# A hybrid decoder trunk on one core: the bias table's DMA in eight pieces, VectorE one tile behind ScalarE at the borders, the norms' sums later

## The chip, the core and the metric
The kernel runs on one core of one Trainium2 chip. The metric is the device time of one execution in microseconds (us). A trace of one execution on the chip is read below; its times count from the span's start.

## The reference
The input is x of 512 tokens by 1024 features in float32. Two layers run, each a half-weighted SwiGLU, a mixer, and another half-weighted SwiGLU, each behind an RMSNorm; the second layer's mixer is B. A final RMSNorm ends it.

```python
def rmsnorm(x, g):
    y = xf * lax.rsqrt(jnp.mean(xf * xf, axis=-1, keepdims=True) + EPS)
    return (y * g).astype(x.dtype)

def swiglu(x, w_in, w_out):                       # D = 1024, D_FF = 2816
    gate, up = jnp.split(x @ w_in, 2, axis=-1)
    return (jax.nn.silu(gate) * up) @ w_out

h = x
for i in range(2):
    h = h + 0.5 * swiglu(rmsnorm(h, norm_g[i, 0]), ffn_w_in[i, 0], ffn_w_out[i, 0])
    hn = rmsnorm(h, norm_g[i, 1])
    y = mixer_a(hn, ..., rel_table) if i == 0 else mixer_b(hn, ...)
    h = h + y
    h = h + 0.5 * swiglu(rmsnorm(h, norm_g[i, 2]), ffn_w_in[i, 1], ffn_w_out[i, 1])
return rmsnorm(h, final_g)
```

Mixer A projects to queries, keys and values of 8 heads and to an index score, keeps the top 128 keys of each query, adds a bias `rel_table[bucket(distance)]` of each head to the logits, and applies softmax and an output projection. Mixer B is a gated MLP with a layer norm and a 128 x 128 spatial product.

## The kernel before
Activations lie transposed: `H[j]`, j = 0 to 7, holds features 128j to 128j+127 on the partitions and the 512 tokens along the row. A matrix product in float32 is made of three products of rounded parts (`mul3`): weights `whi`, `wlo` and activations `xh`, `xl` (or `yh`, `yl`). ScalarE makes a high part, VectorE the low part as value minus high part (lines 173 and 176 for weights, 295 and 296 for activations).

**Weights.** All weights lie in DRAM as one stream of loads of 512 KB (128 rows of 4 KB). SyncE's queue fetches them in order into four buffers `raw` and two `r22`; `_convert_to` makes their parts about two units ahead. Eight tiles of 128 x 128 are one unit. In each FFN the first products are plain; the others are nine blocks of two column pairs by a seven-product scheme, whose four loads are first added and subtracted by VectorE (line 152 adds two of them into `wsum`). [...]

**The start.** During the first FFN's plain products `bias_rows` makes the bias row of each head (`rows`, 8 partitions of 640 floats); line 641 lets GpSimd's DMA queue copy each row 128 times into the DRAM tensor `dist` (8 x 128 x 640 floats). Mixer A reads slanted windows of it some 480 us later (line 818). After the plain products of the first FFN, `scale` and `spread` make the norm's token scale: TensorE sums squares (line 366), VectorE runs twelve small operations of a reciprocal square root (`rsqrt`, lines 282 to 287), TensorE spreads the result over the partitions (line 374), ScalarE reads it (377, 378).

**Borders between stages.** At an FFN's end each output tile j is added to `H[j]` by VectorE (`add`, lines 608 and 609: line 608 reads, and so frees, the PSUM bank), then `finish` calls `prepare(j)` for the next stage: ScalarE makes `xh` and the square, VectorE makes `xl` (296) and adds the square to `sqacc` (307). PSUM banks come in two groups of four, `acc` and `aux`. The next stage's first group again takes four banks of the group that tiles 4 to 7 have just used. In mixers A and B the norm's sum and its reciprocal square root are taken in the wide form (`token_scale`, lines 317 to 324), after step k = 1 of the first group (`hooks={1: scale}`); in the later FFNs `scale` comes after step 3 and `spread` after step 5 of the first group's eight.

**The end.** The last FFN's output product runs in two halves of 256 tokens. Tiles 0 to 3 of a half come from one group in four `aux` banks, tiles 4 to 7 one by one in `acc` banks. `norm_scale` and `norm_rest` of the first half were called from `finish` after tiles 4 and 5 of the second half; `norm_rest` multiplies on GpSimd (line 1104) and writes the output.

Of the kernel before, what the change touches and what calls it, by code (L numbers as in the profile page):

```python
# [19 lines left out]
P = 128  # L20
# [210 lines left out]
def tile_trunk(ctx: ExitStack, tc, specs_out, xT, wst, gT, rel, onehot, bu, bv, lng, lnb, wspT, bsp, out):  # L231
# [21 lines left out]
    def bank(tag="acc"):  # L253
        return psum.tile([P, 512], F32, tag=tag, bufs=4, name=uname(tag))
# [43 lines left out]
    def square(j, s=slice(0, S), adder=nc.vector):  # L298
# [5 lines left out]
        else:  # L304
            sq = small.tile([P, S], F32, tag="s0_512", bufs=1, name=uname("sq"))
            nc.scalar.activation(sq[:, s], H[j][:, s], AF.Square)
            adder.tensor_tensor(acc[0][:, s], acc[0][:, s], sq[:, s], op=ALU.add)

    def prepare(j, norm):
        weigh(j, norm)  # L310
        square(j)

    def token_scale(tag="aux"):

# [63 lines left out]
        nc.scalar.activation(rh, ps, AF.Copy, scale=0.5)  # L378
        return rb, rh

    def ffn(layer, which, norm, finish, begin=None, hooks=None, parts=1):

# [6 lines left out]
        with tc.tile_pool(name=uname("ffn"), bufs=1) as fp:  # L391
# [144 lines left out]
            def hook(k):  # L536
                if hooks:
                    hooks[k]()
                elif k in (3, 5):
                    (scale if k == 3 else spread)()  # L540
                if k > 4 and not hooks:
                    sums(k - 5)

# [30 lines left out]
            for ci, dps in enumerate(CHUNKS):  # L574
                p0 = done
                if ci:
                    Y.clear()
                done += 2 * dps
                if ci == 0:
                    done += PLAIN  # L580
                for i in range(dps):
                    pair = PLAIN + 2 * n_dp
                    between = ()
                    if n_dp == 0:
                        between = [lambda: plain_pairs(rest, g[1], 1 if hooks else 0)]
                    two_pairs(pair, "aux" if n_dp % 2 else "acc", between)
                    n_dp += 1
                flush()
                n_k = done - p0
                tag0 = "aux" if n_dp % 2 else "acc"  # L590
                tag1 = "acc" if n_dp % 2 else "aux"

                def spec_out(k, c, p0=p0):
                    return ("ffn_w_out", (layer, which), (p0 + k) * P, [(0, c * P, P)])

                end = ci == len(CHUNKS) - 1
                if end:
                    W.spool = None
                n = S // (parts if end else 1)
                for at in range(0, S, n):  # L600
                    s = slice(at, at + n)

                    def y_parts(k):
                        return Y[k // 2][0][:, k % 2, s], Y[k // 2][1][:, k % 2, s]

                    def add(j, ps):
                        t = gate_tile()[:, 0]
                        nc.vector.tensor_tensor(t[:, s], ps[:, s], R["h"][:, s], op=ALU.mult)  # L608
                        nc.vector.tensor_tensor(H[j][:, s], H[j][:, s], t[:, s], op=ALU.add)
                        if end:  # L610
                            finish(j, s)

                    first = [bank(tag0) for _ in range(4)]
                    group([ps[:, s] for ps in first], range(4), n_k, spec_out, y_parts)
                    for j in range(4):
                        add(j, first[j])
                    for j in range(4, KD):
                        ps = bank(tag1)
                        single(ps[:, s], j, n_k, spec_out, y_parts)
                        add(j, ps)  # L620
# [7 lines left out]
    def bias_rows(rel_sb, oh_sb, oh):  # L628

        rows = bp.tile([HEADS, TBW], F32, name="rows")  # L630
        rh = bp.tile([BUCKETS, HEADS], F32R, name="rh")
        rl = bp.tile([BUCKETS, HEADS], F32R, name="rl")
        nc.scalar.activation(oh, oh_sb, AF.Copy)
        split(rel_sb, rh, rl)
        for s in (slice(0, TBW // 2), slice(TBW // 2, TBW)):
            ps = bank("aux")
            mm(ps[:HEADS, :TBW // 2], rh, oh[:, s], start=True, stop=False)
            mm(ps[:HEADS, :TBW // 2], rl, oh[:, s], start=False, stop=True)
            nc.vector.tensor_copy(rows[:, s], ps[:HEADS, :TBW // 2])
        d = dram.tile([HEADS, P, TBW], F32, name="dist")  # L640
        nc.gpsimd.dma_start(d, rows.unsqueeze(1).broadcast_to([HEADS, P, TBW]))
        return d

    def mixer_a(dist, next_norm):
        QI0 = 3 * D
# [8 lines left out]
        with ExitStack() as stack:  # L654
# [14 lines left out]

            kw = bank()  # L670
            pq = [bank("aux") for _ in range(4)]
            group([kw] + pq, ["kw"] + [QI0 + P * i for i in range(4)], KD, spec_a, hooks={1: scale})
            rb = R["b"]

            QK = {}
# [234 lines left out]
    def mixer_b(next_norm):  # L910
        with tc.tile_pool(name="mixb", bufs=1) as bp:
# [12 lines left out]
            with tc.tile_pool(name="mixbv", bufs=1) as vp:  # L924
# [10 lines left out]
                for c in range(6):  # L935
                    tag = "aux" if c % 2 else "acc"
                    banks = [bank(tag) for _ in range(NT)]
                    for k in range(KD):
                        wh, wl = W.take(*[("b_w_in", (0,), k * P, [(0, BH + c * 512 + i * P, P)]) for i in range(4)])
                        for t in range(NT):  # L940
                            xh, xl = XH[k][:, t * P:(t + 1) * P], XL[k][:, t * P:(t + 1) * P]
                            mm(banks[t], xh, wh, start=k == 0, stop=False)  # L942
                            mm(banks[t], xl, wh, start=False, stop=False)  # L943
                            mm(banks[t], xh, wl, start=False, stop=k == KD - 1)  # L944
                        if c == 0 and k == 1:
                            R["b"] = token_scale()
                        if c == 0 and k == KD - 1:
                            R["c"] = as_columns(R["b"])
                        if c == 1 and k == 3:
                            for g2 in range(2):  # L950
                                ps = bank("acc")
                                mm(ps, ones, wT.rearrange("p g t -> p (g t)")[:, g2 * 512:(g2 + 1) * 512],
                                   start=True, stop=True)
                                nc.scalar.activation(wsum.rearrange("p g t -> p (g t)")[:, g2 * 512:(g2 + 1) * 512],
                                                     ps, AF.Copy)
# [81 lines left out]
    def into(norm):  # L1037
        return lambda j, s: prepare(j, norm)

    def behind(k):  # L1040
        if k + 1 < KD:
            weigh(k + 1, 0)
        square(k)
        if k == 3:
            dist.append(bias_rows(*table))

    W.first_half()
    weigh(0, 0)
    with tc.tile_pool(name="bias", bufs=1) as bp:
# [4 lines left out]
            table.extend(load_table(oh_sb.bitcast(F32)))  # L1054
            table.append(oh)

        ffn(0, 0, 0, into(1), begin, {k: lambda k=k: behind(k) for k in range(KD)})
    mixer_a(dist[0], 2)
    ffn(0, 1, 2, into(3))
    ffn(1, 0, 3, into(4))  # L1060
    mixer_b(5)
# [5 lines left out]
    def finish(j, s):  # L1067
# [4 lines left out]
                sq.append(small.tile([P, S], F32, tag="s1_512", bufs=1, name="last_sq"))  # L1072
            nc.scalar.activation(sq[0][:, s], H[j][:, s], AF.Square)
        nc.scalar.activation(H[j][:, s], H[j][:, s], AF.Copy, scale=g_sb[:, 6, j:j + 1])
        if s.start and j in (4, 5):
            (norm_scale if j == 4 else norm_rest)(slice(0, s.start), False)

    R = {}

    def norm_scale(s, end):  # L1080
        sums = [bank("aux") for _ in range(nt)]
        for part in (acc[0], sq[0]):
            for t in range(nt):
                at = s.start + t * P
# [5 lines left out]

    def norm_rest(s, end):
        rc = R["c"]
        ps = bank("aux")
        for t in range(nt):
            at = s.start + t * P
            mm(ps[:, at:at + P], rc[:, t:t + 1].broadcast_to([P, P]), ident, start=True, stop=True)
# [8 lines left out]
            queue = nc.gpsimd if not end else nc.sync if j % 2 else nc.scalar  # L1105
            queue.dma_start(out[j, :, s], o)

    ffn(1, 1, 5, finish, parts=parts)
    tail = slice(S - S // parts, S)
    norm_scale(tail, True)  # L1110
    norm_rest(tail, True)
# [51 lines left out]
```

## Time and profile before

| what | value |
|---|---|
| time, median of 3 runs (lowest to highest) | 2173.39 us (2172.07 to 2173.98) |
| time of the profiled execution | 2170.78 us |
| its span, first to last instruction | 2169.0 us |
| mean granted TensorE clock | 0.985 |
| TensorE busy | 2091.4 us, 96% |
| VectorE busy | 1504.3 us, 69% |
| ScalarE busy | 899.8 us, 41% |

The span is what the trace covers; the time of the profiled execution is 1.8 us longer and lies 2.6 us under the median of the three runs. Busy shares are means over stages, so what a stage waits for has to be read in that stage.

### The profile page before, as it was taken

How to read it: one execution, taken by the hardware profiler on the slowest of the kernel's cores; microseconds unless marked ns; L12 is line 12 of the kernel's file. 1: busy time of each engine (PE TensorE's matmuls, PEld its weight loads, DVE VectorE, ACT ScalarE, POOL GpSimd, SP SyncE). 2: the span in 40 equal slices, each digit the busy share in tenths (PEclk: the TensorE clock that was granted, in tenths of full speed). 3: DMA queues.
4: the chain of work that ended last, by engine and by line, in shares of the span. 5: the costliest groups of instructions: out<-in, count | busy, mean ns of one | idle time of the engine just before them, and what ended most of it. 6: DMA issues, size and time to landing. Idle time of an engine off the chain costs nothing.

```text
span 2169.0 us, 29975 instructions
## 1 busy us (share of the span) xinstructions
PE 2091.4 (96%) x12344; PEld 1855.5 (86%) x12344; DVE 1504.3 (69%) x2052; ACT 899.8 (41%) x1163; POOL 91.7 (4%) x76
## 2 busy tenths in 40 slices
PE   7799999899999999998999999999999999999995
PEld 6689998788888999897889998788888888999894
DVE  4868686678667678675968686645846467687675
ACT  4535344343445445353635344322323245344353
POOL 0000000044210000000000000000000000000002
PEclk9799999999999999999999999999999999999998
DMA  6323222232112232222233222422222223222231
GB/s 184 88 99 117 98 98 78 78 110 95 69 68 99 98 117 90 105 98 78 90 105 117 98 98 78 147 88 90 87 104 89 88 88 107 98 98 103 93 117 68
DMA packets 59848, 212.32 MB, mean 98 GB/s; under 512 B 7280, under 2 KB 8368, under 8 KB 59584
## 3 DMA queue, kind: packets, MB, share of 16 engines
q1 hardware_dynamic: 56448, 201.35, 26.6%
q0 software_dynamic: 2688, 8.54, 1.9%
q8 instruction: 96, 1.57, 0.3%
q10 hardware_dynamic: 576, 0.52, 0.1%
q14 instruction: 40, 0.33, 0.0%
HBM read 205.67 MB, written 4.72 MB: 97 GB/s over the span
## 4 chain that ended last, share of the span: by engine, by line
PE 84%; DVE 8%; ACT 4%; issue 2%; DMA 2%; POOL 0%; SPq 0%; POOLq 0%; ACTq 0%; DVEq 0%
PE acc L338 14%; PE acc L339 14%; PE acc L340 14%; PE aux L340 10%; PE aux L338 10%; PE aux L339 10%; DVE wlo L176 2%; DMA raw<-in_wst 2%; ACT whi L173 2%; PE acc L942 1%; PE aux L942 1%; PE aux L943 1%; PE aux L944 1%; PE acc L943 1%; PE acc L944 1%
## 5 line engine op out<-in xcount | busy, mean ns | idle before, releaser
L176 DVE TENSOR_TENSOR wlo<-raw,whi 128x1024 fp32r<-128x1024 f32 (+1 forms) x389 | 471.9, 1218 | 286.6 <-ACT whi L173 282.1
L173 ACT ACTIVATE whi<-raw 128x1024 fp32r<-128x1024 f32 (+1 forms) x416 | 433.5, 1050 | 485.4 <-PE acc L339 216.3
L338 PE MATMUL acc<-xh,whi 128*128 128x256 f32 (+1 forms) x888 | 307.2, 346 | 11.7 <-ACT xh L295 6.3
L339 PE MATMUL acc<-xl,whi 128*128 128x256 f32 (+1 forms) x888 | 297.2, 335 | 0.3 <-DVE xl L296 0.3
L340 PE MATMUL acc<-xh,wlo 128*128 128x256 f32 (+1 forms) x888 | 297.0, 334 | 0.0
L338 PEld LDWEIGHTS acc<-xh,whi 128*128 128x128 f32 x888 | 170.1, 192 | 30.3 <-DVE gate L608 6.5
L338 PE MATMUL aux<-xh,whi 128*128 128x256 f32 (+1 forms) x592 | 191.7, 324 | 1.9 <-ACT rh L378 1.9
L340 PE MATMUL aux<-xh,wlo 128*128 128x256 f32 (+1 forms) x592 | 191.5, 324 | 0.7 <-DVE wlo L176 0.7
L339 PE MATMUL aux<-xl,whi 128*128 128x256 f32 (+1 forms) x592 | 191.3, 323 | 0.0
L338 PE MATMUL acc<-th,whi 128*128 128x256 f32 x640 | 182.5, 285 | 5.9 <-ACT u L490 5.9
L339 PEld LDWEIGHTS acc<-xl,whi 128*128 128x128 f32 x888 | 170.2, 192 | 18.3 <-DVE xl L296 1.5
L340 PEld LDWEIGHTS acc<-xh,wlo 128*128 128x128 f32 x888 | 169.9, 191 | 16.8
L339 PE MATMUL acc<-tl,whi 128*128 128x256 f32 x640 | 182.3, 285 | 0.0
L340 PE MATMUL acc<-th,wlo 128*128 128x256 f32 x640 | 182.1, 285 | 0.0
L338 PE MATMUL acc<-yh,whi 128*128 128x512 f32 (+1 forms) x376 | 143.0, 380 | 2.4 <-ACT whi L173 2.4
L339 PE MATMUL aux<-tl,whi 128*128 128x256 f32 x512 | 145.1, 283 | 0.0
L340 PE MATMUL aux<-th,wlo 128*128 128x256 f32 x512 | 145.1, 283 | 0.0
L338 PE MATMUL aux<-th,whi 128*128 128x256 f32 x512 | 145.1, 283 | 0.0
L340 PE MATMUL acc<-yh,wlo 128*128 128x512 f32 (+1 forms) x376 | 142.5, 379 | 2.3 <-DVE wlo L176 2.3
L340 PE MATMUL aux<-yh,wlo 128*128 128x512 f32 (+1 forms) x376 | 141.7, 377 | 2.3 <-DVE wlo L176 2.3
L338 PE MATMUL aux<-yh,whi 128*128 128x512 f32 (+1 forms) x376 | 141.7, 377 | 1.5 <-ACT whi L173 1.5
L339 PE MATMUL acc<-yl,whi 128*128 128x512 f32 (+1 forms) x376 | 142.2, 378 | 0.0
(261 smaller groups left out, 4396.4 us busy)
## 6 DMA issues: line engine op xcount, KB each, us to landing
raw<-in_wst SPq DMA_DIRECT2D x378, 512.0 KB, 3.2
dist<-rows POOLq DMA_DIRECT2D x1, 2560.0 KB, 55.6
h<-in_xT SPq DMA_DIRECT2D x8, 256.0 KB, 6.6
tb<-dist POOLq DMA_DIRECT2D x8, 256.0 KB, 3.9
bias<-in_bv POOLq DMA_DIRECT2D x1, 1536.0 KB, 7.5
out<-h POOLq DMA_DIRECT2D x8, 128.0 KB, 2.0
raw<-in_wst SPq DMA_DIRECT2D x2, 256.0 KB, 3.5
wT<-in_wspT POOLq DMA_DIRECT2D x1, 512.0 KB, 9.3
```

The costliest lines, as they stand in the source:

```text
L173: self.nc.scalar.activation(hi[:, s], src[:, s], AF.Copy)
L176: self.lo_engine.tensor_tensor(lo[:, s], src[:, s], hi[:, s].bitcast(F32), op=ALU.subtract)
L338: mm(ps, wh, xh, start=first, stop=False, **kw)
L339: mm(ps, wh, xl, start=False, stop=False, **kw)
L340: mm(ps, wl, xh, start=False, stop=last, **kw)
L942: mm(banks[t], xh, wh, start=k == 0, stop=False)
L943: mm(banks[t], xl, wh, start=False, stop=False)
L944: mm(banks[t], xh, wl, start=False, stop=k == KD - 1)
```

## The change
Three things change. The copy of the bias rows to DRAM is cut into eight DMAs, one for each head, which stand in the program ahead of the first FFN's blocks 1 to 8. In `prepare`, ScalarE's two operations of tile j are followed by VectorE's two operations of tile j-1, and the two squares alternate between two buffers. The norms are asked for later: after step 4 instead of 1 in the mixers, after 5 and 7 instead of 3 and 5 in the later FFNs, and in the last FFN the first half's norm moves from tiles 4 and 5 of the second half to steps 2 and 5 of that half's first group, with its banks in `acc`.

```diff
+    behind_it = []
     def prepare(j, norm):
-        weigh(j, norm)
-        square(j)
+        g = g_sb[:, norm, j:j + 1]
+        nc.scalar.activation(XH[j], H[j], AF.Copy, scale=g)
+        if j == 0:
+            acc[0] = small.tile([P, S], F32, tag="acc", bufs=1, name=uname("sqacc"))
+            nc.scalar.activation(acc[0], H[j], AF.Square)
+        else:
+            sq = small.tile([P, S], F32, tag=f"s{j % 2}_512", bufs=1, name=uname("sq"))
+            nc.scalar.activation(sq, H[j], AF.Square)
+        def rest():
+            nc.vector.scalar_tensor_tensor(XL[j], H[j], g, XH[j].bitcast(F32), op0=ALU.mult, op1=ALU.subtract)
+            if j:
+                nc.vector.tensor_tensor(acc[0], acc[0], sq, op=ALU.add)
+        behind_it.append(rest)
+        while len(behind_it) > (j < KD - 1):
+            behind_it.pop(0)()
...
-                elif k in (3, 5):
-                    (scale if k == 3 else spread)()
+                elif k in (5, 7):
+                    (scale if k == 5 else spread)()
...
+                    if aside:
+                        aside(n_dp)
                     two_pairs(pair, "aux" if n_dp % 2 else "acc", between)
...
-                    group([ps[:, s] for ps in first], range(4), n_k, spec_out, y_parts)
+                    group([ps[:, s] for ps in first], range(4), n_k, spec_out, y_parts,
+                          hooks=mids if at else {})
...
-        d = dram.tile([HEADS, P, TBW], F32, name="dist")
-        nc.gpsimd.dma_start(d, rows.unsqueeze(1).broadcast_to([HEADS, P, TBW]))
-        return d
+        return rows, dram.tile([HEADS, P, TBW], F32, name="dist")
+    def spread_bias(rows, d, h):
+        nc.gpsimd.dma_start(d[h:h + 1], rows[h:h + 1].unsqueeze(1).broadcast_to([1, P, TBW]))
...
-            group([kw] + pq, ["kw"] + [QI0 + P * i for i in range(4)], KD, spec_a, hooks={1: scale})
+            group([kw] + pq, ["kw"] + [QI0 + P * i for i in range(4)], KD, spec_a, hooks={4: scale})
...
-                        if c == 0 and k == 1:
+                        if c == 0 and k == 4:
                             R["b"] = token_scale()
...
-        ffn(0, 0, 0, into(1), begin, {k: lambda k=k: behind(k) for k in range(KD)})
+        ffn(0, 0, 0, into(1), begin, {k: lambda k=k: behind(k) for k in range(KD)},
+            aside=lambda i: 0 < i <= HEADS and spread_bias(*dist, i - 1))
...
-        if s.start and j in (4, 5):
-            (norm_scale if j == 4 else norm_rest)(slice(0, s.start), False)
...
-        sums = [bank("aux") for _ in range(nt)]
+        sums = [bank("aux" if end else "acc") for _ in range(nt)]
...
-    ffn(1, 1, 5, finish, parts=parts)
+    head = slice(0, S // parts)
+    ffn(1, 1, 5, finish, parts=parts, mids={2: lambda: norm_scale(head, False), 5: lambda: norm_rest(head, False)})
```

How the program's order moves, at three places. First GpSimd's queue around the copy of the bias rows; `yl` is the buffer that holds the one-hot table, and in brackets stands what semaphore a row waits for (`DMASW0` to `DMASW2` are those of GpSimd's first three DMAs, whose second and third are the first two rows here). Before, and after:

```order
L624 DMA rel_sb<-in_rel 32x8
L625 DMA yl_148<-in_onehot 32x640
L641 DMA dist<-rows 1024x1x640 [waits DVE_49]
L661 MEMSET caus 128x128 [waits DMASW2_49,DMASW3_49,DMASW1_49,DMAHW3_49,DVE_49,DMAHW7_49,PE_49,Activation_49]
L662 AFFINE_SELECT caus<-caus 128x128 [waits Pool_49]
```

```order
L646 DMA rel_sb_150<-in_rel 32x8
L647 DMA yl_15_148<-in_onehot 32x640
L665 DMA dist_264<-rows_250 128x1x640 [waits DVE_49]
L665 DMA dist_264<-rows_250 128x1x640 x4
L665 DMA dist_264<-rows_250 128x1x640 [waits DMASW0_49]
L665 DMA dist_264<-rows_250 128x1x640 [waits DMASW1_49]
L665 DMA dist_264<-rows_250 128x1x640 [waits DMASW2_49]
```

One DMA of 1024 copies has become eight of 128 copies each; only the first still waits for VectorE's copy into `rows`, four wait for nothing, and the last three wait for the ends of the queue's first three loads.

Next VectorE at the border between the second and the third FFN, around tiles 5 and 6 (`h_76`, `h_77`). Before, and after:

```order
L176 TENSOR_TENSOR wlo_8942<-raw_8747,whi_8941 128x1024
L608 TENSOR_TENSOR gate_8959<-acc_8934,rh_5902 128x512
L609 TENSOR_TENSOR h_76<-h_76,gate_8959 128x512
L296 SCALAR_TENSOR_TENSOR xl_93<-h_76,g_sb,xh_85 128x512
L307 TENSOR_TENSOR sqacc_8875<-sqacc_8875,sq_8964 128x512
L176 TENSOR_TENSOR wlo_8981<-raw_8814,whi_8980 128x1024
L608 TENSOR_TENSOR gate_8992<-acc_8967,rh_5902 128x512
L609 TENSOR_TENSOR h_77<-h_77,gate_8992 128x512
L296 SCALAR_TENSOR_TENSOR xl_94<-h_77,g_sb,xh_86 128x512
L307 TENSOR_TENSOR sqacc_8875<-sqacc_8875,sq_8997 128x512
L608 TENSOR_TENSOR gate_9019<-acc_9000,rh_5902 128x512
```

```order
L176 TENSOR_TENSOR wlo_8947<-raw_8754,whi_8946 128x1024
L629 TENSOR_TENSOR gate_8964<-acc_8939,rh_5969 128x512
L630 TENSOR_TENSOR h_76<-h_76,gate_8964 128x512
L323 SCALAR_TENSOR_TENSOR xl_92<-h_75,g_sb,xh_84 128x512
L325 TENSOR_TENSOR sqacc_8881<-sqacc_8881,sq_8935 128x512
L176 TENSOR_TENSOR wlo_8986<-raw_8821,whi_8985 128x1024
L629 TENSOR_TENSOR gate_8997<-acc_8972,rh_5969 128x512
L630 TENSOR_TENSOR h_77<-h_77,gate_8997 128x512
L323 SCALAR_TENSOR_TENSOR xl_93<-h_76,g_sb,xh_85 128x512
L325 TENSOR_TENSOR sqacc_8881<-sqacc_8881,sq_8968 128x512
L629 TENSOR_TENSOR gate_9024<-acc_9005,rh_5969 128x512
L630 TENSOR_TENSOR h_78<-h_78,gate_9024 128x512
```

Behind the addition to `h_76` stood `xl_93` and the square of the same tile; now those of the tile before it (`xl_92`) stand there.

Last VectorE in the last FFN. Before, between tiles 4 and 5 of the second half:

```order
L608 TENSOR_TENSOR gate_18589<-acc_18566,rh_15336 128x256
L609 TENSOR_TENSOR h_75<-h_75,gate_18589 128x256
L307 TENSOR_TENSOR sqacc_18307<-sqacc_18307,sq_18592 128x256
L1088 TENSOR_SCALAR v_18602<-aux_18596 128x1
L1088 TENSOR_SCALAR v_18602<-aux_18597 128x1
L282 TENSOR_SCALAR nwi_18605<-v_18602 128x2
L283 TENSOR_SCALAR nwy_18607<-nwi_18605 128x2
```

And after, between tile 7 of the first half (`h_78`) and the second half:

```order
L629 TENSOR_TENSOR gate_18453<-acc_18434,rh_15403 128x256
L630 TENSOR_TENSOR h_78<-h_78,gate_18453 128x256
L176 TENSOR_TENSOR wlo_18464<-raw_18285,whi_18463 128x1024
L176 TENSOR_TENSOR wlo_18492<-raw_18343,whi_18491 128x1024
L1110 TENSOR_SCALAR v_18513<-acc_18507 128x1
L1110 TENSOR_SCALAR v_18513<-acc_18508 128x1
L282 TENSOR_SCALAR nwi_18516<-v_18513 128x2
L283 TENSOR_SCALAR nwy_18518<-nwi_18516 128x2
```

The first half's reciprocal square root moved from behind the second half's tile 4 to ahead of the second half's tiles, behind two conversions of weights.

## Rows read from the trace of the kernel before

**Rows 1.** the page's head and its first two sections: the span, each engine's busy time (share of the span) and instructions, and the TensorE clock granted in 40 equal slices of the span, in tenths of full speed.
```profile
span 2169.0 us, 29975 instructions
...
PE 2091.4 (96%) x12344; PEld 1855.5 (86%) x12344; DVE 1504.3 (69%) x2052; ACT 899.8 (41%) x1163; POOL 91.7 (4%) x76
...
PEclk9799999999999999999999999999999999999998
```

**Rows 2.** for whom TensorE waited, over the whole span: us in total, times, longest us.
```profile
PE aux L374 <- DVE nwy L287: 15.5, 1, 15.5
PE aux L1096 <- DVE nwy L287: 11.0, 2, 6.4
...
PE acc L320 <- ACT ah L317: 6.0, 1, 6.0
...
PE acc L942 <- DVE gate L608: 5.4, 2, 3.5
```

**Rows 3.** stretches of the span: us, busy us of each engine (x instructions), then the granted TensorE clock (1.00 is 2.4 GHz, 0.50 is 1.2 GHz), the mean busy share of the 16 DMA engines and GB/s.
```profile
10.00:20.00 10.00, 9.71 (x42) 7.43 (x42) 7.30 (x12) 6.60 (x12) 0.00 (x0) 1.00 0.98 379
...
50.00:60.00 10.00, 0.00 (x0) 0.00 (x0) 2.27 (x2) 1.01 (x2) 0.00 (x0) 0.72 0.50 83
60.00:70.00 10.00, 3.33 (x11) 2.88 (x12) 9.24 (x24) 5.73 (x9) 0.00 (x0) 0.50 0.50 85
...
397.00:402.00 5.00, 3.58 (x8) 2.50 (x9) 4.01 (x7) 0.64 (x2) 0.00 (x0) 0.50 0.59 202
1007.00:1013.00 6.00, 4.04 (x9) 2.74 (x10) 4.35 (x8) 2.93 (x5) 0.00 (x0) 0.50 0.26 87
```

**Rows 4.** timeline of TensorE, at the places where it waited (the row at 1390.59 waited for nothing): start us, us, engine, line, operation, tiles [idle before <- who ended it].
```profile
64.76 2.05 PE L374 MATMUL aux<-ident,nwy 128*128 128x128 f32 x8 [15.53 <-DVE nwy L287]
68.72 0.80 PE L338 MATMUL aux<-xh,whi 128*128 128x512 f32 x1 [1.90 <-ACT rh L378]
...
397.69 0.80 PE L320 MATMUL acc<-ah,ones_r 128*128 128x512 f32 x1 [6.03 <-ACT ah L317]
399.22 0.80 PE L321 MATMUL acc<-al,ones_r 128*128 128x512 f32 x1 [0.74 <-DVE al L318]
...
995.65 0.50 PE L338 MATMUL acc<-yh,whi 128*128 128x512 f32 x1 [0.63 <-ACT whi L173]
...
996.91 0.50 PE L340 MATMUL acc<-yh,wlo 128*128 128x512 f32 x1 [0.52 <-DVE wlo L176]
...
1007.14 0.79 PE L338 MATMUL acc<-xh,whi 128*128 128x512 f32 x1 [3.58 <-DVE gate L608]
...
1010.61 0.80 PE L338 MATMUL acc<-xh,whi 128*128 128x512 f32 x1 [1.82 <-DVE gate L608]
...
1390.59 0.60 PE L330 MATMUL aux<-ident,nwy 128*128 128x128 f32 x4
...
2129.88 0.39 PE L338 MATMUL aux<-yh,whi 128*128 128x256 f32 x1 [1.54 <-ACT whi L173]
...
2161.00 1.22 PE L1096 MATMUL aux<-ident,nwy 128*128 128x128 f32 x4 [4.56 <-DVE nwy L287]
```

**Rows 5.** timeline of VectorE, same columns: its wait at the start, the first and the last of the twelve operations of the wide norm in mixer A, one tile's operations at the border at 1003 us, and one operation of the last norm.
```profile
57.73 1.23 DVE L152 TENSOR_TENSOR wsum<-raw,raw 128x1024 f32<-128x1024 f32 x1 [18.17 <-DMA raw<-in_wst]
...
62.28 0.15 DVE L368 TENSOR_SCALAR vcol<-aux 128x4 f32<-128x4 f32 x1
...
400.05 0.69 DVE L323 TENSOR_SCALAR ms<-acc 128x512 f32<-128x512 f32 x1 [0.89 <-PE acc L321]
...
407.52 0.69 DVE L287 SCALAR_TENSOR_TENSOR nwy<-nwt,nwy 128x512 f32<-128x512 f32 x1
...
1003.79 0.75 DVE L296 SCALAR_TENSOR_TENSOR xl<-h,g_sb,xh 128x512 fp32r<-128x512 f32 x1 [0.79 <-ACT xh L295]
...
1005.26 1.22 DVE L176 TENSOR_TENSOR wlo<-raw,whi 128x1024 fp32r<-128x1024 f32 x1
1006.40 0.68 DVE L608 TENSOR_TENSOR gate<-acc,rh 128x512 f32<-128x512 f32 x1
...
1008.60 0.75 DVE L296 SCALAR_TENSOR_TENSOR xl<-h,g_sb,xh 128x512 fp32r<-128x512 f32 x1 [0.79 <-ACT xh L295]
...
2157.08 1.25 DVE L285 TENSOR_TENSOR nwt<-nwy 128x2 f32<-128x2 f32 x1
```

**Rows 6.** DMA queues of the stretch 50:60: packets, MB, share of the time of all 16 engines (q0 is GpSimd's queue, q1 SyncE's).
```profile
q0 software_dynamic: 94, 0.48, 41.7%
q1 hardware_dynamic: 94, 0.35, 8.6%
```

**Rows 7.** DMA issues of the whole span: tiles, queue, operation, times, KB each, median us from issue to landing.
```profile
raw<-in_wst SPq DMA_DIRECT2D x378, 512.0 KB, 3.2
dist<-rows POOLq DMA_DIRECT2D x1, 2560.0 KB, 55.6
```

**Rows 8.** the chain of waits in the stretch 40:110, one piece of it: start us, us, what.
```profile
28.89 28.75 DMA raw<-in_wst
```

**Rows 9.** the DMA issue that writes the tensor dist: line, engine, operation, times, duration ns min/median/max, first and last start us.
```profile
L641 POOL DMA_DIRECT2D dist<-rows x1: 1079/1079/1079, 21.6 to 21.6; - x1
```

**Rows 10.** timeline of SyncE's queue: the two issues of weight loads ahead of the one at 28.89; start us, us, queue, line, operation, tiles.
```profile
22.44 0.33 SPq L105 DMA_DIRECT2D raw<-in_wst  x1
...
28.51 0.33 SPq L105 DMA_DIRECT2D raw<-in_wst  x1
```

More of the change, by code (lines that the diff above doesn't have):

```diff
@@ L379, in scale_rows, with ffn @@
         return rb, rh
-    def ffn(layer, which, norm, finish, begin=None, hooks=None, parts=1):
+    def ffn(layer, which, norm, finish, begin=None, hooks=None, parts=1, aside=None, mids={}):
         NJ = DFF // P
@@ L1044, in behind @@
         if k == 3:
-            dist.append(bias_rows(*table))
+            dist.extend(bias_rows(*table))
     W.first_half()
@@ L1055, in begin @@
             table.append(oh)
-        ffn(0, 0, 0, into(1), begin, {k: lambda k=k: behind(k) for k in range(KD)})
-    mixer_a(dist[0], 2)
+        ffn(0, 0, 0, into(1), begin, {k: lambda k=k: behind(k) for k in range(KD)},
+            aside=lambda i: 0 < i <= HEADS and spread_bias(*dist, i - 1))
+    mixer_a(dist[1], 2)
     ffn(0, 1, 2, into(3))
@@ L1092, in norm_rest @@
         rc = R["c"]
-        ps = bank("aux")
+        ps = bank("aux" if end else "acc")
         for t in range(nt):
```

## The prediction
> **What bounds the kernel now.** The page's head comes first: TensorE is busy 2091.4 of 2169.0 us, and its clock is near full nearly throughout [rows 1]. So VectorE's or ScalarE's time matters only where TensorE waits for it, and the next view is for whom TensorE waits [rows 2]. Four of its entries touch this change: 15.5 us for the norm's scale in the first FFN, 11.0 us in two pieces for the last norms, 6.0 us at mixer A's entry, 5.4 us at mixer B's. Third, the table of stretches: after three of these waits TensorE runs at 0.50 of its clock [rows 3]. A full stream of plain products takes 9.71 us / 42 = 0.231 us each; at 397 us one takes 3.58 / 8 = 0.448, at 1007 us 4.04 / 9 = 0.449. So a stall costs itself and then about 0.22 us for each of the next eight or nine products. The timeline gives each wait its place [rows 4].
>
> The first wait is not made by VectorE's arithmetic. VectorE stands 18.17 us at line 152 for a weight load, and the norm's twelve small operations stand behind that addition in its queue; the first of them starts at 62.28, and TensorE goes on at 64.76 [rows 4, 5]. The load was issued at 28.89 and needed 28.75 us [rows 8], against a median of 3.2 for all 378 loads; the copy of the bias table is in the queues in the meantime, 2560 KB in 55.6 us [rows 7]. From 50 to 60 us both queues moved 94 packets each, strictly by turns; the mean share of the 16 engines was 0.50 [rows 3, 6]. That is eight engines, all busy: 160 us x 0.417 / 94 = 0.71 us for a table packet of 5.1 KB, 160 x 0.086 / 94 = 0.15 us for a weight packet of 4 KB. The table goes at 0.48 MB / 10 us = 48 GB/s.
>
> **The change part by part: the table.** The words say "by heads during the blocks", and this decides the sum. The order of GpSimd's queue shows that nothing holds the pieces until the blocks: the first waits for VectorE's copy as before, four for nothing, three for loads at the queue's start. No piece uses anything a block makes. At about 1.08 us per issue, all eight stand in the queue by about 30 us, the first at 21.6 as now [rows 9]. What does change is their shape. Before, the slowest dimension had 8 entries (one source row each) and eight engines were at work. A piece has 128 copies of one row, as many as the 128 rows of a weight load, and such loads fill all 16 engines (share 0.98 at 379 GB/s) [rows 3]. So I expect the pieces on all 16 engines, one source row at a time, and every packet of a weight load then alternates with a table packet, where before half the engines were free.
>
> [...]
>
> The unknown is how fast one row of SBUF can be read. No row shows it; the bounds are 48 GB/s, if all eight rows shared one ceiling that one row can use alone, and 48 / 8 = 6 GB/s, if each row had its own. I take 24, between them: it is what one engine moves in a full stream (379 / (16 x 0.98) = 24.2) [rows 3], and what a group of four rows got of the 48. Then the table takes 2.62 MB / 24 = 109 us, from about 23.3 to 132 us, and a packet on each of 16 engines 5.12 KB x 16 / 24 = 3.41 us. A weight load is 128 packets, eight on an engine: 8 x (3.41 + 0.15) = 28.5 us each while the table runs. The load that VectorE waits for is third in the queue, behind those issued at 22.44 and 28.51 [rows 10]: 23.3 + 3 x 28.5 = 109 us if the turns are strict, and 132 at the latest, when the table ends. I take 120 instead of 28.89 + 28.75 = 57.6: **+62 us** (51 to 74). Everything behind it (7 us of VectorE up to 64.76, then the half clock) follows as now, and the loads after it come at their own 3.2 us once the table is through.
>
> [...]
>
> **The borders.** At the border into the third FFN VectorE idles 0.79 us in every tile, because line 296 wants a high part that ScalarE has only begun [rows 5]. One tile behind, that operand is ready: 8 x 0.79 = 6.3 us of VectorE's queue go, and line 608, which frees the banks, comes earlier by them. The waits to go are 3.58 + 1.82 for banks and 0.63 + 0.52 for weights' parts queued behind the same idling [rows 4], and the half clock, 9 x 0.218 = 2.0: together 8.5. The 6.3 us of VectorE cover the longest single wait with room. Mixer B's entry shows the same two waits (5.4, longest 3.5) [rows 2]; taken alike, 8.5. Mixer A's entry has 6.03 + 0.74 for the wide norm's input [rows 4], 8 x 0.217 = 1.7 of clock, and I take the same 1.15 for weights: 9.6. Asking for the sum after step 4 instead of 1 is what removes the 6.03. What is late next is the end of that chain: twelve wide operations, from 400.05 to 408.21, 8.2 us [rows 5], must fit in the three steps that remain. In mixer A a step is 15 products, three are 45 x 0.231 = 10.4 us: fits. In mixer B a step is 12 products, three are 8.3 us for 8.2 of chain and some more ahead of it, where before nothing waited (1390.59) [rows 4]: I charge 0.4. In the later FFNs, the small norm two steps later lies under the products of the first group: 0, plus or minus 1. Sum of the borders: 9.6 + 8.5 + 8.1 = **26** (20 to 29).
>
> **The end.** Of the 11.0 us at line 1096 the 6.4 is the first half's norm, asked for between two tiles [rows 2]; at step 5 of a group it has products around it. The 4.56 at 2161 stays [rows 4], but GpSimd's multiplications of the first half end some 11 us earlier, and with them what stretches the last norm's small operations (1.25 us for 128 x 2 at 2157.08, where 128 x 4 took 0.15 at 62.28) [rows 5], two of them on the path: 2 more. Against that, step 2 of the second half must wait for the last square of the first, near the wait of 1.54 for weights at 2129.88 [rows 4], and first-half norm operations now stand ahead of those conversions: 2 to 3 lost. Sum: **5** (2 to 8).
>
> Sum against the profiled execution, span 2169.0 and 1.8 around it: 2170.8 + 62 - 26 - 5 = 2202. It lies 2.6 under the median, so I write 2203.
>
> **Rivals.** *B, the start stays as it is*, the pieces being handled on eight engines at the old rate: nothing in the queue's order speaks against that, the slowest dimension does. 2171 - 31 = 2140. *C, the 48 GB/s can be had from one row:* a packet takes 5.12 x 16 / 48 = 1.71 us, a load 8 x 1.86 = 14.9, the third lands between 23.3 + 44.6 = 68 and 78, the table's end: +15, so 2155. *D, the start's wait vanishes:* a piece on one engine leaves 15 to the weights, or the pieces are held back after all until the blocks have room. Then 15.53 + 1.90 and some 3 of half clock go too [rows 4]: 2171 - 31 - 20 = 2120. *E, one row gives 6 GB/s:* the table lasts 437 us, and each load 8 x 13.8 = 110; far over 2400. The side changes where the third load lands 31 us later, at 89: three loads in 66 us is 2.74 us a pair of packets, 2.6 for the table's, which one row at 82 / 2.6 = 32 GB/s would give. Above that the change is faster, below it slower.
>
> **How the numbers follow.** My forecast has 0.58: the packets by turns are measured, 16 engines are what shape and rows say, but the row's rate is chosen. B 0.13, C 0.12, D 0.13, E 0.04. A measurement of this kernel tells 0.2%, 4 us, from no change. Faster: B, D and nearly all of C, 0.36; same 0.02, the long end of C; slower 0.62. The range leaves out D and E: 2136, B with borders 4 better, to 2235, a row's rate of about 20 (table end at 154, load near 140, +82 less 25 and a few). My forecast's own range is 2185 to 2220.
>
> **What would show it.** In the queues of 50 to 60 us: DMA share near 1.00 instead of 0.50, table packets on GpSimd's queue at about 3.4 us, 24 GB/s. VectorE's wait at line 152 of about 80 us instead of 18.17, TensorE's at line 374 (now 392) of about 77. Table pieces issued within 10 us of 21.6. At the borders no wait of TensorE for line 608's successor, 629, and its clock full. Wrong if the pieces' issue times lie at the blocks, if the share stays at 0.50 with 48 GB/s, or if one row gives over 32 GB/s.

## The result: 2200.3 us, slower by 1.3%

The changed kernel takes 2200.29 us (median of 4 runs, 2199.63 to 2205.22) against 2173.68 before (median of 4, 2172.07 to 2174.23): 26.6 us more. The ratio over all runs is 1.0129, 95% interval 1.0111 to 1.0146. The forecast was 2203.

The profiled execution, below, took 2205.2 us, the longest of the four and 4.9 over their median; that of before lies 2.9 under its median of four. So the two traces differ by 34.5 us where the medians differ by 26.6. The head of its page, as in [rows 1]:

```profile
span 2203.5 us, 29993 instructions
...
PE 2092.6 (95%) x12344; PEld 1856.9 (84%) x12344; DVE 1500.8 (68%) x2052; ACT 899.4 (41%) x1163; POOL 94.8 (4%) x83
```

The work is the same; TensorE is busy 2092.6 us as before. The span has grown by 34.5 us, nearly all of it waiting. For whom TensorE waited (us in total, times, longest), as in [rows 2]; line 392 was 374, 356 was 338, 629 was 608, 965 was 942, 1118 was 1096, and 338 and 339 were 320 and 321:

```profile
PE aux L392 <- DVE nwy L287: 65.7, 1, 65.7
...
PE acc L356 <- ACT whi L173: 5.1, 2, 4.6
PE acc L356 <- DVE gate L629: 3.0, 2, 1.6
PE acc L965 <- DVE gate L629: 3.0, 2, 1.6
...
PE aux L1118 <- DVE nwy L287: 2.4, 1, 2.4
...
PE aux L801 <- DVE wi L770: 1.1, 1, 1.1
PE acc L339 <- DVE al L336: 0.8, 1, 0.8
PE acc L338 <- ACT ah L335: 0.8, 1, 0.8
```

The wait for the first norm went from 15.5 to 65.7 us. The waits at the borders and at the end, 6.0 for mixer A's sums, 5.4 twice for banks and 11.0 for the last norms, went to 1.6, 3.0 twice and 2.4, but a wait of 4.6 us for a weight conversion stands among the new ones.

**The start.** All eight pieces were issued at once (line, engine, operation, times, ns each, first and last start):

```profile
L665 POOL DMA_DIRECT2D dist<-rows x8: 524/524/537, 22.1 to 25.7; - x8
```

That is [rows 9] eight times over, 22.1 to 25.7 us. A stretch after TensorE has stopped, columns as in [rows 3] (the granted clock as a share of full speed; its frequency is in no trace). The share of the 16 DMA engines was 0.50 and is now 1.06:

```profile
50.00:60.00 10.00, 0.00 (x0) 0.00 (x0) 0.00 (x0) 0.00 (x0) 0.00 (x0) 0.59 1.06 48
```

The two DMA queues, from 24 to 37 us (where SyncE's queue, q1, moved nothing and has no row), from 37 to 40, and from 43 to 108, columns as in [rows 6]:

```profile
q0 software_dynamic: 79, 0.32, 85.8%
```

```profile
q0 software_dynamic: 16, 0.08, 95.8%
q1 hardware_dynamic: 15, 0.06, 5.0%
```

```profile
q0 software_dynamic: 456, 1.85, 94.0%
q1 hardware_dynamic: 460, 1.69, 6.3%
```

From 37 us on the queues move packet against packet, 16 and 15, then 456 and 460, and from 43 to 108 the table gets 1.85 MB in 65 us, 28.5 GB/s. From 24 to 37 it is not so: the table moves 79 packets and the weights none, though the first load was issued at 22.92. The first and the third load, issued at 22.92 and 32.87 (tiles, queue, operation, times, KB, us to landing):

```profile
raw<-in_wst SPq DMA_DIRECT2D x1, 512.0 KB, 37.9
...
raw<-in_wst SPq DMA_DIRECT2D x1, 512.0 KB, 75.4
```

So the first landed at 60.8 us and the third at 108.3: 38 us for the first, 47.5 for the two behind it. VectorE's addition that waits for the third load then starts here, in place of 57.73 in [rows 5]:

```profile
108.39 1.22 DVE L152 TENSOR_TENSOR wsum<-raw,raw 128x1024 f32<-128x1024 f32 x1 [68.35 <-DMA raw<-in_wst]
```

**Where the time went, in order of the program.** The start of the same products in both traces, TensorE's timeline of after, columns as in [rows 4]:

```profile
115.42 0.98 PE L392 MATMUL aux<-ident,nwy 128*128 128x128 f32 x3 [65.71 <-DVE nwy L287]
...
1038.67 0.39 PE L356 MATMUL acc<-yh,whi 128*128 128x512 f32 x1
...
1047.05 0.50 PE L356 MATMUL acc<-xh,whi 128*128 128x512 f32 x1 [1.42 <-DVE gate L629]
...
1049.64 0.80 PE L356 MATMUL acc<-xh,whi 128*128 128x512 f32 x1 [1.63 <-DVE gate L629]
...
1427.88 0.33 PE L348 MATMUL aux<-ident,nwy 128*128 128x128 f32 x1
...
2183.56 0.58 PE L356 MATMUL acc<-yh,whi 128*128 128x256 f32 x1 [4.58 <-ACT whi L173]
...
2195.63 0.58 PE L1118 MATMUL aux<-ident,nwy 128*128 128x128 f32 x1 [2.42 <-DVE nwy L287]
```

Against [rows 4] these are late by 115.42 - 64.76 = 50.7 us at the first norm; 1038.67 - 995.65 = 43.0 at the third FFN's border, where before had already waited 0.63, so 43.6 without it; 1049.64 - 1010.61 = 39.0 two columns into the next stage; 1427.88 - 1390.59 = 37.3 behind mixer B's entry; and 2195.63 - 2161.00 = 34.6 at the last norm. So the start lost 50.7 us, mixer A's entry and inside gave back 7.1, the two later borders together 6.3, and the end 2.7.

### The profile page after: what moved, and what is told of

It is laid out like the page before. It is cut to its first block, busy times and chain, and to the rows that moved or that the text cites. A ratio compares the mean times of both kernels' runs of the same rounds, so it can differ in the third digit from the quotient of the medians.

```text
span 2203.5 us, 29993 instructions
## 1 busy us (share of the span) xinstructions
PE 2092.6 (95%) x12344; PEld 1856.9 (84%) x12344; DVE 1500.8 (68%) x2052; ACT 899.4 (41%) x1163; POOL 94.8 (4%) x83
## 4 chain that ended last, share of the span: by engine, by line
PE 78%; issue 8%; DVE 7%; ACT 3%; another core or an unknown queue 3%; POOL 0%; DMA 0%; SPq 0%; POOLq 0%; DVEq 0%; ACTq 0%
PE acc L356 13%; PE acc L357 13%; PE acc L358 13%; PE aux L357 9%; PE aux L356 9%; PE aux L358 9%; DVE wlo L176 1%; ACT whi L173 1%; PE aux L965 1%; PE aux L966 1%; PE aux L967 1%; PE aux L1017 1%; PE acc L965 1%; PE acc L966 1%
```

## The experiments

All ratios are against the kernel before, run beside them on the same chip: 2170.8 us for experiments 1, 2, 3 and 7, 2171.7 for 5, 8, 9 and 10, 2172.4 for 4 and 6. Differences in us between experiments of different groups carry that spread of 1.6 us.

**1. The table's DMA undone, the rest of the change kept** (undo_table). The single DMA stands again behind `rows`, and `aside` is left out.

```diff
-        return rows, dram.tile([HEADS, P, TBW], F32, name="dist")
+        d = dram.tile([HEADS, P, TBW], F32, name="dist")
+        nc.gpsimd.dma_start(d, rows.unsqueeze(1).broadcast_to([HEADS, P, TBW]))
+        return rows, d
```

> The changed kernel with the bias table written by one DMA of 1024 copies, issued where it was before; borders and end as changed. Theory: the start's loss of 50 us is the eight pieces alone, and borders and end gain 16 us as the drift between the two traces says: about 2158 us, TensorE's wait for the first norm back at 15 to 16 us. Rival: the borders and the end gain the 31 us of the forecast and the start lost 57: about 2143.

Measured: 2150.59 us, ratio 0.9909 (0.9894 to 0.9924), 20 us faster than before. TensorE's waits there, columns as above:

```profile
PE aux L392 <- DVE nwy L287: 15.9, 1, 15.9
...
PE acc L356 <- DVE gate L629: 3.0, 2, 1.6
PE acc L967 <- DVE gate L629: 3.0, 2, 1.6
```

The start's wait is the old one, and the borders' waits are after's. So borders and end together are worth 20 us (16 to 23), between the 16 that the two traces gave and the 31 of the forecast. The traced execution of the changed kernel was a long one, so the 16 is a low figure; by medians, experiment 2 less the whole change gives 51.7 - 26.6 = 25. Two rows further down, under the hardware, show one place where two executions differ.

**2. The eight pieces alone, on the kernel before** (table_alone): the new `spread_bias` and `aside`, nothing else.

> The kernel before with the eight pieces alone. Theory: the load that VectorE waits for at the start lands about 50 us later, and nothing else moves: 2173 + 50 = 2223 us, one source row at 28 to 29 GB/s on 16 engines. Rival: part of the 50 us came from the other edits, which put more instructions ahead of the first norm: clearly under 2215.

Measured: 2222.49 us, ratio 1.0241 (1.0226 to 1.0256), 51.7 us slower. TensorE's wait for the first norm is the one of after, to a tenth:

```profile
PE aux L374 <- DVE nwy L287: 65.7, 1, 65.7
```

So the pieces alone make the start's loss, and none of it comes from the other edits. The two halves add: +2.4% and -0.9% make +1.5%, and the whole change measured +1.3%.

**3. Eight rows four partitions apart** (rows_spaced). The kernel before with its single DMA; only the partitions on which the bias rows lie are others: 0, 4, 8, ... 28 instead of 0 to 7.

```diff
-        split(rel_sb, rh, rl)
+        nc.vector.tensor_copy(rx.rearrange("b (h r) -> b h r", r=4), rel_sb.unsqueeze(2).broadcast_to([BUCKETS, HEADS, 4]))
+        split(rx, rh, rl)
...
-        nc.gpsimd.dma_start(d, rows.unsqueeze(1).broadcast_to([HEADS, P, TBW]))
+        nc.gpsimd.dma_start(d, rows[::4].unsqueeze(1).broadcast_to([HEADS, P, TBW]))
```

> The kernel before, its one DMA of 1024 copies kept, but the eight bias rows lie on partitions 0, 4, 8, ... 28 instead of 0 to 7 (the table's matrix product gets a wider left operand for it). [...] Rival: 48 GB/s is what GpSimd's queue or the writing side gives eight engines; the copy stays at 55 us and the time at 2173.

Measured: 2153.47 us, ratio 0.9921 (0.9905 to 0.9938); about 2155 us was expected if the start's wait went. The copy (tiles, queue, operation, times, KB, us to landing), which took 55.6 in [rows 7]:

```profile
dist<-rows POOLq DMA_DIRECT2D x1, 2560.0 KB, 20.8
```

The number of rows, the shape of the copy, the queue and the destination are as before; only where the rows lie has changed, and the same 2560 KB take 20.8 us. So GpSimd's queue and the writing side did not set the 48 GB/s; the place of the source rows did. With it the 15.5 us wait at the first norm is gone. In the changed kernel a piece reads a single row, and with the 16 engines at a share of 1.06 (50 to 60 us) and 94.0% of their time on the table (43 to 108) it goes at 28.5 GB/s.

**4. Rows 16 apart** (rows_16): as 3, with `rows[::16]`.

> As rows_spaced, but the eight rows lie on partitions 0, 16, 32, ... 112. [...]

Measured: 2161.16 us (one run) and a longer copy:

```profile
dist<-rows POOLq DMA_DIRECT2D x1, 2560.0 KB, 30.2
```

30.2 us instead of 20.8: 2.62 MB in 30.2 us are 87 GB/s, against 126 with the rows four apart and 48 with all eight side by side. So the rows' place decides here again, and a larger distance is not simply better; which rows hold each other back the runs do not show. The time that was expected, near 0.992 of the kernel before, did not hold (2161.16 to 2172.4, 0.995): TensorE again waited 2.5 us for the first norm, and VectorE 5.2 us at line 152 for a load, since the loads beside a longer copy came later (the median of the five from 22 to 60 us landed 12.4 us after issue, against 7.4 in experiment 3).

**5. Every row on 16 partitions** (rows128), on undo_table: 128 partitions, each writing eight copies.

```diff
+            nc.gpsimd.dma_start(d.rearrange("h (i r) w -> (h i) r w", r=HEADS),
+                            rows.unsqueeze(1).broadcast_to([P, HEADS, TBW]))
```

> As undo_table (borders and end of the change, one DMA for the table), with every bias row made on 16 partitions, so that 128 partitions each write eight of the 1024 copies. [...] Rival: on 16 engines the copy takes turns with every weight packet, and what it saves in length it costs in the loads beside it: over 0.986.

Measured: 2134.77 us, ratio 0.9832 (0.9817 to 0.9847), 16 us under undo_table (17 by the ratios), where 0.981 to 0.983 was expected if the start's wait went.

```profile
dist<-rows POOLq DMA_DIRECT2D x1, 2560.0 KB, 11.6
```

More than eight engines serve this copy: its queue took 51.0% of the time of all 16 from 22 to 36 us, over what eight could give, as the pieces' queue took 94.0% from 43 to 108. It takes 11.6 us, and the start's wait is gone. So the many engines are no harm in themselves; they are when each of their packets lasts nearly 3 us (an estimate, from 28.5 GB/s, below).

**6. The pieces really held back** (table_late): the change as it is, except that ScalarE's queue issues the pieces, at the same places of the program.

```diff
-        nc.gpsimd.dma_start(d[h:h + 1], rows[h:h + 1].unsqueeze(1).broadcast_to([1, P, TBW]))
+        nc.scalar.dma_start(d[h:h + 1], rows[h:h + 1].unsqueeze(1).broadcast_to([1, P, TBW]))
```

> The changed kernel with its eight pieces issued by ScalarE's queue at the same places of the program, so that they really start one by one in the first FFN's blocks. Theory: each piece still holds all 16 engines at 28 GB/s for 11.4 us and stretches the loads beside it, but a block has some 34 us for four loads of 3.2 us, so it hides, and the start's wait goes: 17 to 20 us under undo_table's 0.991, 0.981 to 0.983. Rival: VectorE waits some 5 us in each block for a stretched load, and 8 x 5 eat the gain: 0.995 or more.

Measured: 2133.78 us, ratio 0.9827 (0.9810 to 0.9843). The issues now lie in the blocks:

```profile
L665 ACTq DMA_DIRECT2D dist<-rows x8: 493/493/585, 83.0 to 315.2; - x8
```

ScalarE reached them in step with the blocks, 83.0 to 315.2 us, where GpSimd, which had nothing to do that would hold it, was through with all eight from 22.1 to 25.7. So what the change says it does is worth 17 us over undo_table, and the same pieces at the wrong moment cost 52. The slow source row is then nearly hidden. In the blocks VectorE does wait for stretched loads, as the rival said, but in three of them and not in eight (us in total, times, longest):

```profile
DVE wsum L152 <- DMA raw<-in_wst: 11.3, 3, 5.3
```

TensorE's only wait there is one of 0.7 us: a block has room for it.

**7. ScalarE's conversion ahead of the tile before** (whi_first), on undo_table. In the FFN's end loop, `add` and with it `prepare` of a tile is written behind the next conversion's `whi` where the next tile begins a new unit.

```diff
                 self.nc.scalar.activation(hi[:, s], src[:, s], AF.Copy)
+                if self.mid:
+                    mid, self.mid = self.mid, None
+                    mid()
...
+                    def add_mid(j, ps):
+                        if end and parts == 1 and j < KD - 1 and W.at + n_k > LOAD:
+                            W.mid = lambda: add(j, ps)
+                        else:
+                            add(j, ps)
```

> As undo_table, and at the FFNs' ends ScalarE converts the next unit of weights ahead of the high part and the square of the tile before, wherever the next tile uses a new unit. Theory: the border's pace of 4.81 us a tile is a loop, VectorE's add, ScalarE's high part, square and conversion, VectorE's low part, and back to the add; taken apart, three waits of 1.0 us of VectorE go at each border and with them TensorE's waits of 1.4 and 1.6 us for banks and the half clock behind them: 8 to 10 us under undo_table. Rival: VectorE is simply full at the borders, and the idle 1.0 us moves elsewhere as the 0.79 did: within 2 us of undo_table.

Measured: 2143.80 us, ratio 0.9877 (0.9862 to 0.9891), 6.8 us under undo_table. VectorE at the border of the third FFN, no wait left, 3.73 us from one `wlo` to the next:

```profile
986.32 1.22 DVE L180 TENSOR_TENSOR wlo<-raw,whi 128x1024 fp32r<-128x1024 f32 x1
...
990.05 1.22 DVE L180 TENSOR_TENSOR wlo<-raw,whi 128x1024 fp32r<-128x1024 f32 x1
```

And TensorE's first columns of the next stage, which waited 1.4 and 1.6 us and now go on:

```profile
993.61 0.39 PE L360 MATMUL acc<-xh,whi 128*128 128x512 f32 x1
...
994.52 0.50 PE L360 MATMUL acc<-xh,whi 128*128 128x512 f32 x1
```

So VectorE was not full there; it stood in a loop. The gain is somewhat under the 8 to 10 expected, because the half clock that I counted for both borders stood at only one of them in undo_table: 0.66 granted from 998 to 1003 us at the third FFN, 1.00 at mixer B's entry.

**8. The end's multiplications on VectorE** (tail_dve), on undo_table.

```diff
-                nc.gpsimd.tensor_tensor(o, o, rb[:, s], op=ALU.mult)
+            if not end:
+                nc.vector.tensor_tensor(o, o, rb[:, s], op=ALU.mult)
...
+        if s.start and j in (4, 5, 6):
+            for _ in range(3):
+                rest_of_head and rest_of_head.pop(0)()
```

> As undo_table, but the first half's eight multiplications at the end are VectorE's, three behind each of the second half's tiles 4, 5 and 6, and not GpSimd's during tiles 0 to 3. Theory: GpSimd's multiplications stretch VectorE's operations beside them (1.2 and 2.1 us where 0.43 and 1.23 is usual), and that makes TensorE's waits of 2.7 and 1.4 us for weights in the second half; both go, the eight multiplications of 0.4 us lie in VectorE's gaps: 3 to 5 us under undo_table (0.989 of the kernel before). Rival: VectorE's added work pushes the last adds back as much: within 1.5 us of it.

Measured: 2148.80 us, ratio 0.9899 (0.9884 to 0.9914): 1.8 us under undo_table, inside the uncertainty. The mechanism is there and its gain is not: TensorE's waits for ScalarE's conversions fell from 3.2 to 2.1 us in all, and at the last sums a wait grew that was 1.0 in undo_table:

```profile
PE aux L1112 <- DVE sqacc L307: 4.2, 1, 4.2
...
PE acc L356 <- ACT whi L173: 2.1, 2, 1.6
```

VectorE's added work pushed its last additions back, as the rival said.

**9. Mixer A's parts earlier** (early_split), on undo_table.

```diff
-            group([kw] + pq, ["kw"] + [QI0 + P * i for i in range(4)], KD, spec_a, hooks={4: scale})
+            group([kw] + pq, ["kw"] + [QI0 + P * i for i in range(4)], KD, spec_a, hooks={2: halves, 3: scale})
```

> As undo_table, but mixer A's sum of squares is cut into its two parts after step 2 of the first group and multiplied after step 3, not both after step 4. Theory: TensorE's waits of 0.8 and 0.85 us for the parts go, since ScalarE and VectorE make them during a step; the scale is ready 3.4 us earlier, and the 1.1 us wait at the index weights goes too: 1.6 to 3 us under undo_table. Rival: the parts queue behind a conversion of weights that waits for TensorE in any case: no change beyond 1 us.

Measured: 2151.42 us, ratio 0.9906 (0.9889 to 0.9922), no difference from undo_table. In its trace the three waits in mixer A are gone, but the time does not show the 2 us; in the profiled execution they are lost again at mixer B's entry, where the granted clock fell to 0.64 and was 1.00 in undo_table, and at the end, where the wait for a conversion was 4.6 us and 2.7 in undo_table. Both also differ between undo_table and the changed kernel, which are the same program there. Inconclusive.

**10. All together** (best): rows128, whi_first, tail_dve and early_split.

> rows128, whi_first, tail_dve and early_split together. If the four gains are at four places and add: 0.991 of the kernel before less 18, 7, 4 and 2 us, 0.977 (about 2120 us). Rival: what one takes away at the end or a border the next wait gives back: over 0.981.

Measured: 2119.26 us, ratio 0.9762 (0.9747 to 0.9776). TensorE is busy 98% of its span. It beats the kernel before by 2.4% and the changed one by 3.6%. The gains at the table and the border conversions are shown one by one; those of 8 and 9 are not.

## Why the prediction held, and where it did not

**What bounds the start: right.** The pieces were issued at once, they kept all 16 engines busy (a share of 1.06 from 50 to 60 us), from 37 us on each load alternated with them, and VectorE's queue stood at line 152 with the norm behind it. Experiment 2 shows that this alone costs 52 us, and experiment 6 that issue at the blocks would have gained instead; the words of the change were no guide here, the waits in the queue's order were. The sum's last step has a slip: 2202 and 2.6 make 2204 or 2205, not 2203.

**The start's size: +50.7 for +62,** just under the stated 51 to 74. Two terms were off, against each other. The row's rate was taken as 24 GB/s and measured 28.5 (43 to 108 us), so by estimate a full table packet lasts 5.12 x 16 / 28.5 = 2.9 us instead of 3.41 and a load 8 x 3.0 = 24 instead of 28.5. That 24 was a choice: no run shows that four of the eight rows share a limit. By strict turns from 23.3 us on, the third load would then have landed at 96 us. It landed at 108, because the turns began only at 37 us: until then 79 packets of the table went and none of the weights. From 37 us three loads of 24 us end at 109, and the two later loads did take 47.5 us together. The prediction's strict case gave 109 too, with a row too slow and turns from 23.3 us on: that was luck. The "120" was the middle between the strict case and the table's end at 132; the table ended at 118, since its row was faster.

**The rivals.** B (start as it is) and D (no stall) fell with the wait of 65.7. C fell with 28.5 GB/s for one row instead of 48. E fell by the same number. The side was decided where the prediction put it: under 32 GB/s slower.

**The borders: 26 forecast, 13.4 in the trace of after.** The step that failed is "8 x 0.79 = 6.3 us of VectorE's queue go". It counted VectorE's idle time before line 296 as if nothing else closed the loop. VectorE at the same tile as in [rows 5], and ScalarE beside it:

```profile
1041.50 0.68 DVE L629 TENSOR_TENSOR gate<-acc,rh 128x512 f32<-128x512 f32 x1
1042.21 0.69 DVE L630 TENSOR_TENSOR h<-h,gate 128x512 f32<-128x512 f32 x1
1042.82 0.74 DVE L323 SCALAR_TENSOR_TENSOR xl<-h,g_sb,xh 128x512 fp32r<-128x512 f32 x1
1043.49 0.69 DVE L325 TENSOR_TENSOR sqacc<-sqacc,sq 128x512 f32<-128x512 f32 x1
1045.17 1.23 DVE L176 TENSOR_TENSOR wlo<-raw,whi 128x1024 fp32r<-128x1024 f32 x1 [0.99 <-ACT whi L173]
1046.31 0.68 DVE L629 TENSOR_TENSOR gate<-acc,rh 128x512 f32<-128x512 f32 x1
```

```profile
1042.94 0.73 ACT L314 ACTIVATE xh<-h,g_sb 128x512 fp32r<-128x512 f32 x1 [2.62 <-DVE h L630]
1043.57 0.62 ACT L320 ACTIVATE sq<-h 128x512 f32<-128x512 f32 x1
1044.09 1.04 ACT L173 ACTIVATE whi<-raw 128x1024 fp32r<-128x1024 f32 x1
```

The wait of 0.79 is gone, and one of 0.99 stands before `wlo` instead; from addition to addition a tile takes 1046.31 - 1041.50 = 4.81 us; before, from one line 296 to the next, 1008.60 - 1003.79 = 4.81. ScalarE begins its high part only when VectorE's addition has ended, then does the square and only then the conversion, whose low part stands in VectorE's queue ahead of the next tile's addition. By the starts: 1041.50 line 629, 1042.21 line 630, 1042.94 `xh`, 1043.57 the square, 1044.09 `whi`, 1045.17 `wlo`, 1046.31 line 629 again. In before the same chain already set the pace, its conversion and its low part the same 1.08 us apart (1004.18, and 1005.26 in [rows 5]), so taking away the wait in front of line 296 could not shorten it:

```profile
1004.18 1.04 ACT L173 ACTIVATE whi<-raw 128x1024 fp32r<-128x1024 f32 x1
```

The chain runs through both engines, and shifting VectorE's two operations, which were not on it, only moves where VectorE stands. The gain of the border was that of the tiles without a conversion, and of the bank waits 1.42 of 3.58 and 1.63 of 1.82 stayed. The half clock behind them, 2.0 us of the forecast at each of these two borders, stayed too (0.64 granted at mixer B's entry, in the last section), so the prediction's sign, no wait for line 629 and a full clock, did not come. Experiment 7 opens the loop and takes both. Cost of an operation at its engine was the wrong measure; the loop's length was the right one.

**Mixer A: 9.6 forecast, 7.1 measured.** The 6.03 did go. What the sum left out is the wait at the new place: the parts of the sum are made at step 4 behind a conversion that itself waits for TensorE, 0.8 and 0.8 us, and the index weights wait 1.1 more. I had asked only whether the chain ends in time, not whether it begins when TensorE asks.

**The end: 5 forecast, 2.7 measured.** (The terms named there make 5.4 to 6.4.) The 6.4 went. The multiplications on GpSimd that move forward were said to stop stretching the last norm, and did: its wait fell from 4.56 to 2.42. The 2 to 3 us set down for step 2 were a wait of 0.6. What the prediction does not name is what the multiplications do at their new place: they stretch the second half's additions. VectorE, ScalarE and one of GpSimd's multiplications there:

```profile
2175.45 1.19 DVE L307 TENSOR_TENSOR sqacc<-sqacc,sq 128x256 f32<-128x256 f32 x1 [0.48 <-ACT sq L306]
...
2183.54 2.12 DVE L176 TENSOR_TENSOR wlo<-raw,whi 128x1024 fp32r<-128x1024 f32 x1 [0.33 <-ACT whi L173]
```

```profile
2181.60 0.42 ACT L306 ACTIVATE sq<-h 128x256 f32<-128x256 f32 x1 [2.32 <-DVE h L630]
```

```profile
2175.59 0.75 POOL L1126 TENSOR_TENSOR h<-h,last_rb 128x256 f32<-128x256 f32 x1
```

An addition of 128 x 256 takes 1.19 us and 0.43 at 2187.01, where GpSimd has finished; the 0.76 between the two is about one multiplication, 0.75. A low part takes 2.12, elsewhere 1.22. In experiment 8, where GpSimd has no multiplication at this place, the addition takes 0.43 (2120.18) and the low part 1.23 (2125.07). What holds VectorE up beside a multiplication, no run shows. ScalarE waits for the stretched additions and makes the next `whi` only at 2182.47, behind the square of 2181.60. So TensorE's 4.58 us at 2183.56 came with it, which the prediction set at nothing, and the ten us after it run at half clock:

```profile
2184.00:2194.00 10.00, 7.45 (x32) 6.69 (x31) 6.92 (x17) 3.70 (x8) 2.50 (x4) 0.50 0.11 39
```

**The sum.** +50.7 - 13.4 - 2.7 = +34.6 in the profiled execution, +26.6 by the medians; forecast was +31 from +62 - 26 - 5. The total was right to about 4 us against either, with its parts off by 11, 13 and 2: the start's error and the borders' took each other away. That the total came so near was luck.

## What to carry to other kernels

A DMA placed later in the program did not start later here by its place alone: the same eight pieces went out at 22.1 to 25.7 us from GpSimd's queue, whose engine had nothing to hold it, and at 83.0 to 315.2 from ScalarE's, whose engine was at work in the blocks; read the waits on that queue before counting on the place. A copy that replicates a few rows of SBUF was as slow as the partitions it read from (28.5 GB/s from one row; 2560 KB in 11.6 us from all 128), and while the one row was read, from 37 us on, the transfers beside it took turns with it, packet against packet (456 and 460 from 43 to 108 us); spread the source rows over the partitions first. Where two engines wait for each other in turn, add up the loop: moving operations that were not on it moved only the wait (4.81 us a tile before and after, 3.73 with the loop opened).

## What the hardware showed beyond that

**The clock behind the same waits.** At mixer B's entry undo_table and the changed kernel have the same two waits (1.4 and 1.6 us, banks), and the clock that follows differs: first undo_table, then the changed kernel, columns as in [rows 3].

```profile
1349.50:1354.50 5.00, 3.37 (x15) 2.44 (x15) 4.96 (x9) 3.19 (x5) 1.34 (x3) 1.00 0.37 125
```

```profile
1402.00:1407.00 5.00, 3.37 (x9) 2.41 (x10) 4.96 (x8) 3.03 (x5) 1.17 (x3) 0.64 0.31 105
```

1.00 granted in the one, 0.64 in the other, and by that 15 products against 9 in 5 us. At waits of this size the half clock comes or does not, and it explains some of the 4 us by which 20 (experiment 1) and 16 (the traces) differ. More of them lie at the end, where the wait for a conversion was 4.6 us in the changed kernel's trace and 2.7 in undo_table's. What tips either is open.

**The queue that came first got everything.** From 24 to 37 us no packet of the weights moved, then one went against one of the table. The first load of weights was issued at 22.92 (SyncE's queue in after), ahead of the table's first packets at 23.2:

```profile
22.92 0.33 SPq L105 DMA_DIRECT2D raw<-in_wst  x1
```

The first piece, issued at 22.06, landed 14.1 us later, at 36.1, and the weights began behind it. The runs don't show why; it was not tried.
